# Gate matrices of an expert layer: a new loop order in their eviction, and a new placing of the products with u around them

## The chip, the cores and the metric

The kernel runs on one core of a Trainium2 chip. The metric is device time in microseconds of one launch. The kernel before was timed three times: 2685.2, 2690.42 and 2691.59 us, median 2690.42.

## The reference, cut to what matters

Two transformer layers work on 256 latent tokens and 256 context tokens of width 1024. Each has attention heads and then an expert network of 16384 experts (PEER). Layer 1 runs its experts on the 256 latent tokens alone. This is the expert part:

```
q = (xb @ wq).reshape(T, HEADS=8, 2, 128)
s = einsum('thpd,pnd->thpn', q, sub_keys)          # 2 x 128 scores per head
sv, si = top_k(s, 16)
cand = sv[:, :, 0, :, None] + sv[:, :, 1, None, :] # 256 pairs per head
fv, fp = top_k(cand, 16)
eidx = take_along_axis(cidx, fp)                   # 16 experts per token and head
g = softmax(fv)
a = einsum('thkd,td->thk', take(u, eidx), xb)
wgt = gelu(a) * g
out = einsum('thk,thkd->td', wgt, take(v, eidx))
```

An expert's number is i * 128 + j, so that a token's chosen experts and their softmax weights can be written as a 128 by 128 gate matrix, mostly zero.

## The kernel before, in words

In both layers most token tiles take a dense way through the experts. Layer 0 has four tiles of 128 tokens: three go the dense way (nd = 3), and the fourth gathers single rows of u and v by GpSimd while the main loop runs. Layer 1 has two tiles, both dense (nd = 2).

The dense way has four stages, all in `peer` (lines 991 to 1208) and what it calls.

1. **Scores** (`route_scores`, line 808). Sixteen query blocks are projected with wq, multiplied with the sub-keys, and VectorE takes the top 16 of each. SyncE loads the weights into six raw buffers (tag w) and every one is split into a rounded high and a low part: ScalarE casts (line 166), VectorE subtracts (line 167). A product of two split operands is three matmuls (lines 190 to 192). Weight loads follow one list, `start_weights`; `w_end` bounds how far down it `take` may load ahead. In layer 0 it ends behind the adaLN blocks that the filler uses.
2. **Prologue.** `route` (line 856, six steps per tile, almost all VectorE) finds a tile's 128 experts (i, j) and weights. `gates` (line 919) then makes the gate matrices of 128 tokens, eight tokens at a time: VectorE compares with an iota for the one-hot tiles oh (line 946) and weighs them into og (lines 949, 952; ScalarE does the rest of og, line 956), TensorE multiplies the pairs (line 970), and ScalarE evicts each PSUM tile p of four tokens t by 128 j into `stage`, which is laid out [128 rows, 128 j, 32 t] (line 973). SyncE stores a full stage to G in DRAM by two transfers of 1024 KB (line 977).
3. Meanwhile **chunks** of u run: `achunk` (line 1027) multiplies 128 experts of u with all dense tokens, 24 matmuls in the split form, followed by a Gelu into `ring` (line 1039). In layer 1 every fifth chunk is taken unsplit (line 212). `lag` chunks (27 in layer 0, 47 in layer 1) are done before the main loop. A chunk loads u up to three chunks ahead and splits one ahead. The adaLN products (line 244) are a filler in layer 0.
4. **Main loop**, 128 rounds: loads v and G, does one more chunk of u while there are any, multiplies ring with the gates (line 1167), splits the result w and v, and accumulates w times v (lines 190 to 192 on vs, w) in PSUM.

How many chunks go where in the prologue is paced by weights: a route step of any tile counts RW = 3, a half step of gates 1, and chunk i is issued once `i * tot < done * (lag - TAIL[l])`. Counted through, layer 0 issues 3 chunks during the first tile's route steps, 20 during gates, and 4 behind them; layer 1 issues 6, 36 and 5. The chunks left over come before the filler is drained, before the last pool is closed and before the main loop's `load_g(0)`, `load_v(0)`, `load_v(1)`.

[...]

Of the kernel before, what the change touches and what calls it, by code (L numbers as in the profile page):

```python
# [15 lines left out]
AF = mybir.ActivationFunctionType  # L16
# [12 lines left out]
LAG = (27, 47)  # L29
LATE = 12  # L30
RW = 3
ADA_LOAD = 3
AV1 = 2
EARLY = (2, 1)
# [3 lines left out]
GPIPE = 2  # L38
FSTEP = 3
GSCALE = 16384.0  # L40
TAIL = (4, 5)
RSTEP = 4
U_AHEAD = (1, 3)
RAWQ = (3, 6, 9, 12, 15)
# [45 lines left out]
class Kernel:  # L90
# [34 lines left out]
    def start_weights(self):  # L125
        A = self.A
        q = []
        for half in range(2):
            for v in (0, 1):
                q += self.ada_specs(0, v)[4 * half:4 * half + 4]  # L130
            q += [(("win", b), A["ab_in"][b], 1024, True) for b in ((0, 1), range(2, 14))[half]]
        q += [(("av", b), A["ab_v"][b], 1024, True) for b in range(4)]
        for v in (2, 3, 4):
            q += self.ada_specs(0, v)
        q += [(("wout0", b), A["w_out"][0, b], 1024, True) for b in range(8)]
        q += [(("wq0", b), A["wq"][0, b], 1024, True) for b in range(16)]
        q += self.ada_specs(0, 5)
        for v in range(AV1):
            q += self.ada_specs(1, v)
        self.w1_at = len(q)  # L140
        q += [(("cdin", 0), A["cd_in"][0], 1024, True)]
        q += [(("ckv", b), A["cd_ckv"][b], 768, True) for b in range(4)]
        q += [(("cdin", b), A["cd_in"][b], 1024, True) for b in range(1, 9)]
        q += [(("dv", b), A["cd_v"][b], 1024, True) for b in range(4)]
        q += [(("uq", 0), A["uq_n"], 1024, True), (("uq", 1), A["uq_r"], 512, True), (("ukv", 0), A["ukv"], 1024, True)]
        for v in range(AV1, 6):
            q += self.ada_specs(1, v)
        q += [(("wout1", b), A["w_out"][1, b], 1024, True) for b in range(8)]
        q += [(("wq1", b), A["wq"][1, b], 1024, b not in RAWQ) for b in range(16)]
        self.wq_, self.wl, self.wsp, self.wt = q, 0, 0, 0  # L150
        self.wraw, self.whi = {}, {}
        self.w_end = self.w1_at

    def ada_specs(self, l, v):
        return [(("ada", l, b), self.A["ada_w"][l, b], 1024, False) for b in range(8 * v, 8 * v + 8)]
# [649 lines left out]
        for v, y, p in zip(V, b, X):  # L805
            nc.vector.max_index(p[:, 8:16], v[:, 8:16], y)

    def route_scores(self, l, T, nd, hh, hl):

        nc = self.nc  # L810
        kt = self.wn.t("rt", [128, 2, 128], name="kt")
        nc.sync.dma_start(kt, self.A["keys"][l])
        sv = [self.wn.t("rt", [128, 2, 2, 16, 16], name="sv") for _ in range(nd)]
        sd = self.dp.tile([128, 16, 128], F, name="sd") if T > nd else None
        qs = {}
        c = T * 128
        ready = {}

        def project(b):
            p = self.proj_t(("wq%d" % l, b), hh, hl, c=c)  # L820
            q = self.wn.t("rt", [128, 512], name="q")
            nc.scalar.copy(q[:, :c], p[:, :c])
            qs[b] = q

        def scores(b):
            q = qs.pop(b)
            p = self.ps([128, 4, 128])
            for t in range(T):
                nc.tensor.matmul(p[:, t, :], q[:, t * 128:(t + 1) * 128], kt[:, b % 2, :], start=True, stop=True)
            s = self.wn.t("rt", [128, 2, 4, 128], name="sc")  # L830
            nc.scalar.copy(s[:, 0, :T, :], p[:, :T, :])
            if T > nd:
                nc.sync.dma_start(sd[:, b, :], s[:, 0, nd, :])
            ready[b] = s

        def top(b):
            s = ready.pop(b)
            self.top16([x[:, 0, 0, b, :] for x in sv], [x[:, 0, 1, b, :].bitcast(U32) for x in sv],
                       [s[:, 0, t, :] for t in range(nd)], [s[:, 1, t, :] for t in range(nd)])

        routes = [self.route(x, lambda n, s, d=F: self.wn.t("rt", s, d, name=n)) for x in sv]
        for b in range(18):
            if b == 10:
                for r in routes[:EARLY[l]]:
                    next(r)
            if b < 16:
                project(b)
            if 0 <= b - 1 < 16:
                scores(b - 1)
            if 0 <= b - 2 < 16:  # L850
                top(b - 2)
        return routes, sd
# [67 lines left out]
    def gates(self, go, ti, G):  # L920

        nc = self.nc
        p = self.ps([128, 3, 128])
# [35 lines left out]
        def product():  # L959
            n, oh, og_ = pend.pop(0)  # L960
            part, q = n // 4, n % 4
            if q == 0:
                stages[part] = self.wn.t("stage", [128, 128, 32])
            stage = stages[part]
            for half in range(2):
                p = self.ps([128, 4, 128])
                for k in range(4):
                    for w in range(2):
                        g, b = half * 2 + k // 2, k % 2
                        nc.tensor.matmul(p[:, k, :], oh[:, 0, g, :, b], og_[:, w, g, :, b], start=(w == 0),  # L970
                                         stop=(w == 1))
                c4 = q * 8 + half * 4
                nc.scalar.activation(stage[:, :, c4:c4 + 4].rearrange("p i t -> p t i"), p, AF.Copy,  # L973
                                     scale=1.0 / GSCALE)
            if q == 3:
                for c in range(2):
                    nc.sync.dma_start(G[16 * c:16 * c + 16, :, 4 * ti + part, :, :].rearrange("c p i t -> p c (i t)"),
                                      stage[:, 64 * c:64 * c + 64, :].rearrange("p (c i) t -> p c (i t)", i=4))
# [9 lines left out]
    def peer(self, l, xs, sq, nd):  # L988
# [13 lines left out]
        self.m.close()  # L1002
        rg = Phase(self.tc, "ring%d" % l, {"ring": lag + 2})
        self.wn = Phase(self.tc, "win%d" % l, W_BUFS)
        routes, sd = self.route_scores(l, T, nd, hh, hl)
        G = self.dp.tile([32, 128, 4 * nd, 4, 32], F, name="G%d" % l)
        self.rt = []
        ustr, usp, useen, vstr, gstr, ring = {}, {}, set(), {}, {}, {}
# [1 line left out]
        def load_u(i):  # L1010
            if i < NCH and i not in useen:
                useen.add(i)
                ustr[i] = self.wraw_t()
                nc.sync.dma_start(ustr[i], A["uT"][l, i].rearrange("p k e -> p (k e)"))
# [4 lines left out]
        def split_u(i):  # L1019
            if i < NCH and i not in usp and not raw(i):  # L1020
                h, o = self.wsp_t(), self.wsp_t()
                self.split(ustr.pop(i), h, o)
                usp[i] = (h, o)

        def achunk(i):
            for k in range(U_AHEAD[1] + 1):
                load_u(i + k)
            for k in range(U_AHEAD[0] + 1):
                split_u(i + k)
            p = self.ps()  # L1030
            if raw(i):
                self.product8(p[:, c], ustr.pop(i))
            else:
                uh, ul = usp.pop(i)
                for k in range(8):
                    b = slice(k * 128, (k + 1) * 128)
                    self.mm3(p[:, c], uh[:, b], ul[:, b], hh[:, k, c], hl[:, k, c], k == 0, k == 7)
            ring[i] = rg.t("ring", [128, TD])
            nc.scalar.activation(ring[i], p[:, c], AF.Gelu)


        def prologue():
            for _ in routes[0]:
                yield RW
            for t in range(nd):
                nxt = routes[t + 1] if t + 1 < nd else None
                for n, _ in enumerate(self.gates(self.rt[t], t, G)):
                    yield 1
                    if nxt and n % RSTEP == RSTEP - 1 and next(nxt, True) is None:
                        yield RW  # L1050
                if nxt:
                    for _ in nxt:
                        yield RW

# [5 lines left out]

        filler = fill()
        i = 0
        tot = (6 * nd - EARLY[l]) * RW + nd * (32 + 2 * GPIPE)
        done = 0
        for n, w in enumerate(prologue()):
            done += w
# [2 lines left out]
            while i < lag and i * tot < done * (lag - TAIL[l]):  # L1069
                achunk(i)  # L1070
                i += 1
        while i < lag:
            achunk(i)
            i += 1
        for _ in filler:
            pass
        self.wn.close()
# [63 lines left out]
        def load_v(i):  # L1141
            if i < NCH:
                vstr[i] = mn.t("v", [128, 1024])
                nc.sync.dma_start(vstr[i], A["v"][l, i * 128:(i + 1) * 128, :])

        def split_v(i):
            if i < NCH:
                h, o = mn.t("vs", [128, 1024], R), mn.t("vs", [128, 1024], R)
                self.split(vstr[i], h, o)
                vstr[i] = (h, o)  # L1150

        def load_g(i):
            if i < 32:
                gstr[i] = mn.t("g", [128, 4 * nd, 4, 32])
                nc.sync.dma_start(gstr[i], G[i])
# [34 lines left out]
            return min(256, -(-256 * (at(j + 1) - at(LATE)) // (at(NCH - 3) - at(LATE))))  # L1190

        nu = 0
        load_g(0)
        load_v(0)
        load_v(1)
        split_v(0)
        weight(0)
        for j in range(NCH):
# [277 lines left out]
```

## Time and profile before

| what | value |
|---|---|
| median of three runs | 2690.42 us |
| profiled execution | 2690.64 us |
| its span, first to last instruction | 2688.9 us |
| TensorE busy (PE) | 2574.6 us, 96% |
| VectorE busy (DVE) | 1870.6 us, 70% |
| ScalarE busy (ACT) | 1266.4 us, 47% |
| mean granted TensorE clock | 0.981 |

How to read it: an engine is busy while one of its instructions executes. TensorE's matmuls overlap in the records, so the step from one start to the next tells its pace better than a matmul's duration. An idle stretch of an engine is put down to the event that ended it. [...]

### The profile page before, as it was taken

The page shows a single profiled execution, that of the slowest core. Times are in us where ns is not written, and L with a number is a line of the kernel's source. Part 1 is how long each engine was busy: PE and PEld are TensorE (multiplying, and loading weights), DVE is VectorE, ACT ScalarE, POOL GpSimd, SP SyncE. Part 2 cuts the span into 40 slices and gives each one's busy share as a digit, 9 for nine tenths or more (in the row PEclk, how much of TensorE's full clock was granted, in tenths as well). Part 3 has the DMA queues.
Part 4 walks back from the last instruction along what each step waited for, and adds up shares of the span by engine and source line. Part 5 has one row for each costly group of instructions (what it writes and reads, how often), then busy time and mean ns, then how long its engine had stood idle before and what let it go on. Part 6 is the DMA issues. An engine that isn't in the chain of part 4 may idle for free. (4 is left out here: it accounts for less than half of the span.)

```text
span 2688.9 us, 43066 instructions
## 1 busy us (share of the span) xinstructions
PE 2574.6 (96%) x16265; PEld 2248.1 (84%) x16265; DVE 1870.6 (70%) x3862; ACT 1266.4 (47%) x2201; POOL 526.7 (20%) x534
## 2 busy tenths in 40 slices
PE   7999998989999999999999997999999999999998
PEld 6866787878999999999999777768999899999986
DVE  4267689886967777777777756477987665555555
ACT  4255335996333333333333334454599444444444
POOL 0000000000045555556666631010000000000000
PEclk9999999989999999999999998999999999999999
DMA  7362324877688888888888863464478876666355
GB/s 295 104 220 99 110 89 143 283 236 243 233 312 311 310 314 312 300 319 314 304 301 306 277 227 110 156 218 144 136 248 247 314 256 212 211 211 212 126 196 180
DMA packets 240977, 614.15 MB, mean 228 GB/s; under 512 B 18384, under 2 KB 102608, under 8 KB 240768
## 3 DMA queue, kind: packets, MB, share of 16 engines
q1 hardware_dynamic: 203904, 477.17, 52.0%
q0 software_dynamic: 36864, 134.23, 14.2%
q8 instruction: 127, 2.08, 0.3%
q14 instruction: 82, 0.67, 0.1%
HBM read 558.90 MB, written 52.43 MB: 227 GB/s over the span
## 5 line engine op out<-in xcount | busy, mean ns | idle before, releaser
L166 ACT CAST ws<-w 128x1024 fp32r<-128x1024 f32 (+1 forms) x327 | 342.9, 1050 | 632.7 <-PE p L191 584.0
L167 DVE TENSOR_TENSOR ws<-w,ws 128x1024 fp32r<-128x1024 f32 (+1 forms) x327 | 397.4, 1216 | 262.9 <-ACT ws L166 256.7
L166 ACT CAST vs<-v 128x1024 fp32r<-128x1024 f32 x256 | 269.5, 1053 | 506.5 <-PE p L191 506.5
L191 PE MATMUL p<-vs,w 128*128 128x512 f32 x1280 | 502.3, 393 | 5.2 <-DVE vs L167 5.2
L190 PE MATMUL p<-vs,w 128*128 128x512 f32 x1280 | 499.6, 391 | 5.0 <-ACT vs L166 5.0
L192 PE MATMUL p<-vs,w 128*128 128x512 f32 x1280 | 501.3, 392 | 0.0
L190 PE MATMUL p<-hh,ws 128*128 128x384 f32 (+1 forms) x1304 | 462.2, 355 | 6.3 <-ACT ws L166 2.9
L192 PE MATMUL p<-hh,ws 128*128 128x384 f32 (+1 forms) x1304 | 455.7, 350 | 1.6 <-DVE ws L167 1.6
L191 PE MATMUL p<-hl,ws 128*128 128x384 f32 (+1 forms) x1304 | 456.6, 350 | 0.1
L167 DVE TENSOR_TENSOR vs<-v,vs 128x1024 fp32r<-128x1024 f32 x256 | 312.7, 1222 | 152.2 <-ACT vs L166 149.2
L190 PE MATMUL p<-hp,ws 128*128 128x256 f32 x1032 | 295.7, 287 | 1.8 <-ACT ws L166 1.1
L192 PE MATMUL p<-hp,ws 128*128 128x256 f32 x1032 | 293.0, 284 | 0.8 <-DVE ws L167 0.8
L191 PE MATMUL p<-hp,ws 128*128 128x256 f32 x1032 | 293.4, 284 | 0.0
L191 PEld LDWEIGHTS p<-vs,w 128*128 128x128 f32 x1280 | 241.2, 189 | 53.7 <-DVE vs L167 8.4
L192 PEld LDWEIGHTS p<-vs,w 128*128 128x128 f32 x1280 | 240.9, 188 | 53.3 <-DVE w L1169 2.4
L190 PEld LDWEIGHTS p<-vs,w 128*128 128x128 f32 x1280 | 241.1, 189 | 51.4 <-ACT vs L166 5.3
L190 PEld LDWEIGHTS p<-hh,ws 128*128 128x128 f32 x1304 | 247.9, 190 | 24.7 <-ACT ws L166 4.4
L191 PEld LDWEIGHTS p<-hl,ws 128*128 128x128 f32 x1304 | 247.7, 190 | 14.7 <-DVE hl L367 0.3
L192 PEld LDWEIGHTS p<-hh,ws 128*128 128x128 f32 x1304 | 247.3, 190 | 13.1 <-DVE ws L167 2.0
L1139 DVE SCALAR_TENSOR_TENSOR acc<-gr,ga,acc 128x1024 f32<-128x1024 f32 x128 | 164.2, 1283 | 100.8 <-DMA gr<-in_v,ix 100.0
L1134 DVE SCALAR_TENSOR_TENSOR gr<-gr,hn 128x1024 f32<-128x1024 f32 x128 | 156.0, 1222 | 107.7 <-DMA gr<-in_u,ix 107.4
L310 POOL TENSOR_TENSOR rso<-rsm,mhalf 128x1 f32<-128x1 f32 x30 | 20.2, 673 | 1055.0 <-DVE rsm L308 1041.6
(273 smaller groups left out, 4118.5 us busy)
## 6 DMA issues: line engine op xcount, KB each, us to landing
w<-in_uT SPq DMA_DIRECT2D x256, 512.0 KB
v<-in_v SPq DMA_DIRECT2D x256, 512.0 KB
w<-in_ada_w SPq DMA_DIRECT2D x96, 512.0 KB
G<-stage SPq DMA_DIRECT2D x40, 1024.0 KB
g<-G SPq DMA_DIRECT2D x32, 768.0 KB
w<-in_wq SPq DMA_DIRECT2D x32, 512.0 KB
g<-G SPq DMA_DIRECT2D x32, 512.0 KB
w<-in_w_out SPq DMA_DIRECT2D x16, 512.0 KB
```

The costliest lines, as they stand in the source:

```text
L166: self.nc.scalar.copy(hi, raw)
L167: self.nc.vector.tensor_tensor(lo, raw, hi.bitcast(F), op=OP.subtract)
L190: m(out, lh, rh, start=start, stop=False)
L191: m(out, lh, rl, start=False, stop=False)
L192: m(out, ll, rh, start=False, stop=stop)
L310: nc.gpsimd.tensor_tensor(o, m, self.mhalf[:, :n], op=OP.pow)
L1134: nc.vector.scalar_tensor_tensor(t, t, 1.0, hn, op0=OP.mult, op1=OP.mult, accum_out=ga[:, 0, n:n + 1])
L1139: nc.vector.scalar_tensor_tensor(acc, t, ga[:, 0, n - 128:n - 127], acc, op0=OP.mult, op1=OP.add)
```

## The change

- Line 973's eviction writes `stage` in its own order, four tokens side by side for each j, and reads the PSUM tile with a stride of 128 words from token to token. Before, it read the PSUM tile in order and wrote single words 32 words apart.
- `route_scores` calls `ahead(b)` after each projection: from b = 14 on it loads one chunk of u per step, and at b = 17 it splits chunk 0. In layer 0 the weight list is bounded at `late_at`, ahead of the filler's adaLN blocks, until the scores are done.
- Route steps of the first tile count 8 (layer 0) and 5 (layer 1) in the pacing, and TAIL of layer 1 is 8. Counted through, layer 0 issues 6 chunks in the first tile's route steps, 18 during gates and 3 behind them; layer 1 issues 9, 30 and 8.
- The chunks left over are issued after the filler's drain, the closing of the pool, `load_v(0)`, `load_v(1)` and `load_g(0)`, in this order; the two v loads come ahead of `load_g(0)`.

```diff
+RW0 = (8, 5)
-TAIL = (4, 5)
+TAIL = (4, 8)
 def start_weights
         q += [(("wq0", b), A["wq"][0, b], 1024, True) for b in range(16)]
+        self.late_at = len(q)
         q += self.ada_specs(0, 5)
...
-        self.w_end = self.w1_at
+        self.w_end = self.late_at
 def route_scores(self, l, T, nd, hh, hl, ahead)
             if b < 16:
                 project(b)
+            ahead(b)
 def gates
-                nc.scalar.activation(stage[:, :, c4:c4 + 4].rearrange("p i t -> p t i"), p, AF.Copy,
+                nc.scalar.activation(stage[:, :, c4:c4 + 4], p.rearrange("p t i -> p i t"), AF.Copy,
                                      scale=1.0 / GSCALE)
 def peer
-        routes, sd = self.route_scores(l, T, nd, hh, hl)
...
+        def ahead(b):
+            if b >= 14:
+                load_u(b - 14)
+            if b == 17:
+                split_u(0)
+
+        routes, sd = self.route_scores(l, T, nd, hh, hl, ahead)
+        if l == 0:
+            self.w_end = self.w1_at
...
             for _ in routes[0]:
-                yield RW
+                yield RW0[l]
...
-        tot = (6 * nd - EARLY[l]) * RW + nd * (32 + 2 * GPIPE)
+        tot = (6 - EARLY[l]) * RW0[l] + 6 * (nd - 1) * RW + nd * (32 + 2 * GPIPE)
...
-        while i < lag:
-            achunk(i)
-            i += 1
         for _ in filler:
             pass
...
-        load_g(0)
         load_v(0)
         load_v(1)
+        load_g(0)
+        while i < lag:
+            achunk(i)
+            i += 1
         split_v(0)
         weight(0)
```

## Rows read from the trace of the kernel before

**Rows 1.** The page's first part: busy time, share of the span, instructions.
```profile
PE 2574.6 (96%) x16265; PEld 2248.1 (84%) x16265; DVE 1870.6 (70%) x3862; ACT 1266.4 (47%) x2201; POOL 526.7 (20%) x534
```

**Rows 2.** Layer 0 by stretch: start:end length, busy of PE PEld DVE ACT POOL, PEclk, DMA.
```profile
411.00:440.00 29.00, 20.01 (x168) 17.98 (x171) 27.82 (x135) 11.65 (x16) 0.53 (x1) 0.87 0.39 131
440.00:634.00 194.00, 170.99 (x1634) 153.95 (x1626) 160.44 (x338) 179.13 (x344) 2.10 (x4) 0.92 0.75 234
634.00:656.50 22.50, 20.39 (x113) 20.07 (x114) 12.26 (x14) 11.98 (x18) 0.00 (x0) 0.92 0.89 303
```

**Rows 3.** Groups of ScalarE instructions from 440 to 634 us: busy us, mean ns | idle before.
```profile
L973 ACT ACTIVATE stage<-p 128x512 f32<-128x512 f32 x96 | 98.0, 1135 | 2.3 <-PE p L970 2.3
L956 ACT ACTIVATE og<-oh,gl 128x128 f16<-128x128 f16 x192 | 62.9, 445 | 2.6 <-DVE oh L946 2.4
L166 ACT CAST ws<-w 128x1024 fp32r<-128x1024 f32 x18 | 19.2, 1073 | 1.6 <-PE p L191 1.6
L1039 ACT ACTIVATE ring<-p 128x384 f32<-128x384 f32 x20 | 10.0, 502 | 4.0 <-PE p L192 4.0
```

**Rows 4.** Groups of VectorE instructions from 440 to 634 us.
```profile
L946 DVE TENSOR_TENSOR oh<-io,ijgt 128x2048 f16<-128x2048 f16 x48 | 58.5, 1218 | 7.2 <-ACT ijgt L928 7.2
L949 DVE TENSOR_TENSOR og<-oh,ijgt 128x1024 f16<-128x1024 f16 x48 | 32.9, 686 | 0.6
L167 DVE TENSOR_TENSOR ws<-w,ws 128x1024 fp32r<-128x1024 f32 x20 | 24.4, 1221 | 15.7 <-ACT ws L166 15.7
L952 DVE TENSOR_TENSOR og<-oh,ijgt 128x512 f16<-128x512 f16 x48 | 20.1, 418 | 0.0
```

**Rows 5.** TensorE's waits in three stretches (411:440, then 440:634, then 1904:2097).
```profile
PE p L228 <- DVE ijg L916: 6.3, 1, 6.3
...
PE p L970 <- DVE og L949: 10.3, 7, 3.2
PE p L970 <- ACT og L956: 6.6, 4, 1.8
...
PE p L190 <- ACT vs L166: 5.0, 1, 5.0
PE p L228 <- DVE ijg L916: 2.9, 1, 2.9
```

**Rows 6.** First and last of ten matmuls of a layer 0 chunk: start us, us.
```profile
430.56 0.33 PE L192 MATMUL p<-hh,ws 128*128 128x384 f32 x1
...
432.12 0.34 PE L192 MATMUL p<-hh,ws 128*128 128x384 f32 x1
```

**Rows 7.** Groups by form, ScalarE over the span, then VectorE from 411 to 660 us.
```profile
L973 ACT ACTIVATE stage<-p 128x512 f32<-128x512 f32 x160 | 164.1, 1143 | 2.5 <-PE p L970 2.3
L478 ACT COPY PT<-p 128x512 f32<-128x512 f32 x32 | 18.7, 586 | 8.0 <-PE p L228 7.7
...
L900 DVE CAST xs<-sv 128x128 f16<-128x128 f32 x3 | 0.8, 258 | 0.0
L889 DVE CAST sv<-sv 128x128 f32<-128x128 uint32 x3 | 0.7, 219 | 0.0
```

**Rows 8.** Layer 1 by stretch, columns as in Rows 2.
```profile
1904.00:1927.00 23.00, 20.03 (x140) 18.68 (x140) 22.96 (x114) 10.28 (x17) 0.00 (x0) 1.00 0.34 115
1927.00:2077.00 150.00, 146.76 (x1367) 141.30 (x1366) 123.95 (x231) 140.99 (x268) 0.00 (x0) 0.99 0.74 230
2077.00:2097.00 20.00, 14.95 (x99) 13.87 (x98) 9.08 (x12) 9.01 (x15) 0.00 (x0) 0.95 0.97 332
```

**Rows 9.** SyncE's queue before layer 1's main loop, then the chain's G load (start, us).
```profile
2076.90 3.50 SPq L977 DMA_DIRECT2D G<-stage  x2
2080.49 4.05 SPq L1014 DMA_DIRECT2D w<-in_uT  x2
2084.64 0.42 SPq L1155 DMA_DIRECT2D g<-G  x1
...
2084.64 6.58 DMA g<-G
```

More of the change, by code (lines that the diff above doesn't have):

```diff
@@ L806, in top16, with route_scores @@
             nc.vector.max_index(p[:, 8:16], v[:, 8:16], y)
-    def route_scores(self, l, T, nd, hh, hl):
+    def route_scores(self, l, T, nd, hh, hl, ahead):
         nc = self.nc
```

## The prediction

> **What bounds the kernel now.** I read the page's first part, then busy time by stretch over both prologues, then the groups and waits inside them. TensorE is busy for 96% of the span [rows 1] and the change takes no matmul away, so only time in which TensorE waits or runs slowly can be won. In the stretches by time the reader should look for two things: which engine is full where TensorE is not, and the granted clock. [...] VectorE's largest idle time is its wait for ScalarE's casts, 15.7 us [rows 4]. TensorE waits for og, 10.3 us for VectorE's part and 6.6 us for ScalarE's [rows 5]. In layer 1's gates TensorE is nearly full, 146.8 of 150 us, with ScalarE at 141.0 just behind [rows 8]. The other losses are single stalls: 6.3 us in layer 0 and 2.9 us in layer 1, where the last chunk of the route steps is done and the first tile's ijg is not, and 5.0 us where layer 1's main loop starts and its first v split has waited on ScalarE behind the G data [rows 5, 9].
>
> **The eviction.** The instruction keeps its 512 elements. A copy of the same size on the same engine, PSUM to SBUF with both sides in order, takes 0.586 us, the eviction 1.143 [rows 7]: the difference of 0.557 us is what single words scattered 128 bytes apart cost. After the change the written side has four adjacent words at a time; the read side hops 512 bytes each element, and no row shows a strided read of PSUM. Bounds: 0.586 from below (the copy); from above 1.70, today's time with the same 0.557 us added once more, since nothing in the trace excludes that a hopping read costs more than a hopping write. The nearest row of a strided read is on VectorE in SBUF: 128 elements read 64 bytes apart take 0.258 us against 0.219 in order [rows 7], 0.04 us more, so 0.16 us for 512. I take 0.70 us, nearest to the copy, a little under 0.586 + 0.16 = 0.75, since that row is of another engine and memory.
>
> The trace shows that scattered single words cost, and not whether four-word runs cure it. [...]
>
> **Layer 0, gates.** ScalarE: 96 x (1.135 - 0.70) = 41.8 us less; two chunks fewer lie in the gates (18 for 20), each a cast of 1.07 and a Gelu of 0.50 [rows 3], 3.1 us. It falls to 179.1 - 41.8 - 3.1 = 134 us. VectorE does the same gates and routes and two subtractions of 1.22 us fewer [rows 4]: 158 us. TensorE: nine matmuls of a chunk start within 1.56 us, 0.173 us apart [rows 6], a chunk of 24 is 4.2 us, so 171.0 x 0.92 - 2 x 4.2, about 149 us at full clock. VectorE is late next, and that is what limits the gain: with ScalarE anywhere under some 0.95 us per eviction (179.1 - 3.1 - 96 x 0.18 = 158) VectorE is the bound. Of the 33.6 us that it idles now I leave 8: half of the wait of 7.2 us on ijgt, which is a chain through TensorE, and a quarter of that on the casts. So the gates last 166 us in place of 194.
>
> Their start moves back by the three more chunks in the route steps. VectorE is full there (27.8 of 29.0 us [rows 2]), so their splits of 1.22 us come on top: 3.7 us. TensorE's 12.6 us for them go into its 6.3 us stall and the wait around it, and cost nothing more unless they outlast the chain, by which the gates would start up to 5 us later; the range holds that. Behind the gates one chunk less is left over, 4.2 us. The stretch from 634 to the first v product at 656.5 is otherwise kept. Layer 0: 3.7 + 166 - 194 - 4.2 = -28 us.
>
> **Layer 1.** The 2.9 us stall is filled by three more chunks, each by estimate 2.8 us (two thirds of layer 0's columns). They overshoot the chain by some 5 us, but as TensorE is the bound of the gates that only orders its work otherwise. In the gates ScalarE has 64 x 0.44 = 28 us less and six chunks fewer, VectorE seven; TensorE's 3.2 us of waits there go [rows 8], and the clock losses of 0.01 x 150 + 0.05 x 20 = 2.5 us that follow the stalls. At the main loop's start the last G store is issued at 2076.90, the G load at 2084.64, and it lands 6.58 us later [rows 9], 14.3 us in all; eight chunks left over are 22 us and cover it, where five with their loads in front did not, so the 5.0 us go. Sum 2.9 + 3.2 + 2.5 + 5.0 = 13.6; I keep 1.6 for waits that reappear, so -12 us.
>
> **The loads.** The u loads in the projections put chunks 0 to 3 ahead of adaLN blocks in the same six buffers. Both come some 6 us apart before they are used, so I take 0, between 2 us gained at the first chunk and 3 us lost at the first filler step. The two v loads now stand ahead of `load_g(0)`, and the leftover chunks' u loads behind it. [...] The last chunk of the prologue has loaded three more chunks (12.5 us of TensorE in layer 0, 8.4 in layer 1), and a later one may be planned ahead of the G load, so I take 0; the price without that cover is the first rival's.
>
> **Sum.** -28 - 12 = -40 us on the profiled execution's 2690.64 us (span 2688.9 and 1.7 around it), which is 0.2 us over the median: 2650 us. Its own range is 2634 to 2668.
>
> **Rivals.**
> 1. *Starved leftover chunks.* The eviction is fast, but u loads stuck behind `load_g(0)` leave TensorE dry. SyncE is held 2084.64 - 2076.90 = 7.7 us [rows 9], then v, v, G and u, some 2 MB at 332 GB/s [rows 8], 6 to 7 us more: 14 us against 8.4 of cover in layer 1 and 12.5 in layer 0, so 6 + 2 us and a slow clock after each, some 4 us. 2662 us. [...] Against: the u issue of 2080.49 stands between G store and G load today, so loads that are ready do get in.
> 2. *The read pays what the write paid.* The eviction stays near 1.14 us and only the placing counts. Layer 0: gates start 3.7 later, ScalarE has 3.1 less in them, one chunk less behind: -3.6. Layer 1: gates start 3 x 2.8 - 2.9 = 5.5 later, ScalarE's bound shrinks by 6 x 1.45 = 8.7, three more chunks behind add 8.4 and hide 5.0: about 0. 2687 us.
> 3. *The read pays more*: the eviction at 1.70 us. ScalarE is the bound of both gates, so every 0.1 us adds 0.1 x 160 = 16 us [rows 7]: -3.4 + 89 gives 2776 us. It decides from 1.21 us on, where the 3.4 us are spent and 8 more are lost. For it: no row shows a read that hops 512 bytes. Against: the one strided read that a row shows costs 0.3 ns per element [rows 7].
>
> **How the numbers follow.** Forecast 0.60, rival 1 0.13, rival 2 0.17, rival 3 0.10. A difference under 0.3%, 8 us, can't be told from no change: within it lies most of rival 2, 0.12, its rest is faster. Faster 0.60 + 0.13 + 0.05 = 0.78, same 0.12, slower 0.10. The range starts at 2632, where VectorE idles nowhere in layer 0's gates (8 us more) and nearly nothing reappears, and ends at 2692, past rival 2; it leaves out rival 3 and a little below.
>
> **What the profile after would show.** The eviction group under 0.95 us, near 0.70. Layer 0's gates at some 166 us with VectorE fuller than ScalarE. No wait of TensorE for ijg in either layer, six and nine chunks ahead of the first transposes. The first v product of layer 1 without a wait for vs. Wrong if the eviction is 1.1 us or more; if it is fast and the gates of layer 0 still last over 180 us; or if TensorE waits for u in the leftover chunks.

## The result, and the profile after

The change made the kernel faster, by less than forecast: 2664.55 us median (2661.32 to 2667.70, four runs) beside 2691.01 of the kernel before on the same chip, 26.5 us, ratio 0.9893 [0.9871, 0.9915]. Forecast were 2650 us and 40 us. In a second set of runs it was 2668.97 beside 2693.58, ratio 0.9918 [0.9892, 0.9945]. The profiled execution is the 2661.32 one.

First the page's busy time, then the eviction's group over the span (line 973 before is 976 now; VectorE's and ScalarE's lines 166/167, 946, 949 are 168/169, 949, 952; TensorE's gate products, 970 before, are 973 now).

```profile
PE 2553.3 (96%) x16265; PEld 2232.6 (84%) x16265; DVE 1868.8 (70%) x3862; ACT 1201.5 (45%) x2201; POOL 514.6 (19%) x534
```

```profile
L976 ACT ACTIVATE stage<-p 128x512 f32<-128x512 f32 x160 | 86.4, 602 | 6.3 <-PE p L973 6.0
```

ScalarE lost 64.9 us of work against [rows 1], and the eviction's group alone lost 77.7: 602 ns for one where [rows 7] have 1143. It is now within 16 ns of the plain copy's 586 in the same rows. The other groups of ScalarE last as long as before; that the sum fell by less than the group is no new work. Instructions of ScalarE overlap in the trace, and the page counts such time once: by count and mean of its groups they last 1448.6 us in sum in the kernel before and 1358.4 now, 90.2 us less, and the busy times are 1266.4 and 1201.5.

The stretches of both prologues come next, in the columns of [rows 2]: layer 0's route steps, gates and the part behind them, then the same of layer 1.

```profile
409.60:437.00 27.40, 27.40 (x211) 26.63 (x210) 27.40 (x122) 11.92 (x15) 0.53 (x1) 1.00 0.52 168
437.00:612.00 175.00, 153.60 (x1576) 138.20 (x1575) 157.73 (x336) 140.22 (x342) 2.10 (x4) 0.95 0.82 251
612.00:633.20 21.20, 18.14 (x109) 17.82 (x109) 9.46 (x10) 10.35 (x16) 0.00 (x0) 0.99 1.01 336
1888.00:1915.60 27.60, 27.58 (x205) 26.55 (x205) 27.24 (x112) 13.25 (x20) 0.00 (x0) 1.00 0.43 153
1915.60:2041.00 125.40, 122.69 (x1202) 118.54 (x1201) 114.95 (x224) 107.06 (x257) 0.00 (x0) 1.00 0.79 245
2041.00:2067.00 26.00, 26.00 (x194) 25.16 (x193) 12.66 (x19) 11.58 (x19) 0.00 (x0) 1.00 1.02 360
```

Against [rows 2] the fullest engine of layer 0's gates has changed: before, it was ScalarE, busy for 179.1 of 194 us, 98.0 of them with the evictions [rows 3]; now VectorE is busy for 157.7 of 175 us, ScalarE for 140.2. In layer 1 [rows 8] TensorE is now busy for all but 2.7 us of 179, and its granted clock (PEclk, as a share of full speed) is 1.00 in all three stretches.

Now the waits in layer 0 from the end of the scores to the main loop, first TensorE's, then VectorE's (one answer for 437:612, one for 612:640), then two of VectorE's in the kernel before (440:634 and 634:660). The figures are us in total, times, longest us.

```profile
PE p L973 <- DVE og L952: 8.5, 8, 2.7
PE p L246 <- DMA w<-in_ada_w: 4.8, 2, 4.1
...
PE p L192 <- ACT w L1177: 3.1, 1, 3.1
```

```profile
DVE mod L275 <- PE p L270: 6.5, 2, 6.0
DVE oh L949 <- ACT ijgt L931: 4.8, 2, 2.7
DVE ws L169 <- ACT ws L168: 1.7, 2, 1.4
...
DVE ws L169 <- ACT ws L168: 9.9, 4, 3.6
DVE vs L169 <- ACT vs L168: 4.6, 1, 4.6
```

```profile
DVE mod L273 <- PE p L268: 3.8, 1, 3.8
...
DVE ws L167 <- ACT ws L166: 14.1, 4, 6.7
```

TensorE's wait for ijg [rows 5] is gone. VectorE's wait for casts inside the gates fell from 15.7 us [rows 4] to 1.7, but one for TensorE grew from 3.8 to 6.5 us, and at the main loop's door VectorE waits for casts as long as before, 14.5 us beside 14.1.

For the comparisons the trace was cut at events: start of the first score product, its end, the first transpose of ijg, the last gate product, the first v product. Each length is the difference of two start times, in us.

| | before | after | after, 2nd | eviction only | placing only |
|---|---|---|---|---|---|
| layer 0, scores | 93.8 | 91.4 | 91.4 | 93.8 | 91.4 |
| to the first ijg transpose | 22.8 | 27.5 | 27.5 | 23.0 | 27.5 |
| to the last gate product | 190.7 | 174.4 | 174.3 | 174.2 | 193.8 |
| to the first v product | 27.1 | 21.8 | 21.6 | 23.0 | 24.4 |
| layer 0, main loop | 955.9 | 961.8 | 965.3 | 970.7 | 965.6 |
| layer 1, scores' end to first v | 190.0 | 178.8 | 179.7 | 181.4 | 191.4 |

Profiled execution against profiled execution 29.3 us went: layer 0's scores 2.4, from there to the first v product 16.9, layer 1's prologue 11.2, its main loop 1.7; the start of the kernel 3.9 shorter, layer 0's main loop 5.9 longer and the way from there to layer 1's scores 0.7 longer.

### The profile page after: what moved, and what is told of

It is laid out like the page before. It is cut to its first block, busy times and chain, and to the rows that moved or that the text cites. A ratio compares the mean times of both kernels' runs of the same rounds, so it can differ in the third digit from the quotient of the medians.

```text
span 2659.5 us, 43074 instructions
## 1 busy us (share of the span) xinstructions
PE 2553.3 (96%) x16265; PEld 2232.6 (84%) x16265; DVE 1868.8 (70%) x3862; ACT 1201.5 (45%) x2201; POOL 514.6 (19%) x534
## 5 line engine op out<-in xcount | busy, mean ns | idle before, releaser
L193 PEld LDWEIGHTS p<-vs,w 128*128 128x128 f32 x1280 | 241.3, 189 | 58.1 <-DVE vs L169 12.8
L1143 DVE SCALAR_TENSOR_TENSOR gr<-gr,hn 128x1024 f32<-128x1024 f32 x128 | 156.0, 1222 | 107.4 <-DMA gr<-in_u,ix 107.0
```

The source lines that it names most:

```text
L193: m(out, lh, rl, start=False, stop=False)
L1143: nc.vector.scalar_tensor_tensor(t, t, 1.0, hn, op0=OP.mult, op1=OP.mult, accum_out=ga[:, 0, n:n + 1])
```

## The experiments

**The changed kernel once more.** The same file.

> The changed kernel once more, as a measure for the others. Profiled before at 2661.3 us with 29 us less than the kernel before: 17 us between the end of layer 0's scores and its first v product, 11 us in layer 1's same stretch, but 6 us more lost in layer 0's main loop, where VectorE waits for gathered rows of v. If that loss belongs to the change, the main loop of layer 0 again takes about 962 us against 956; if it is scatter of the gathers, it falls anywhere between 950 and 965. Time 2660 to 2668.

Measured: 2668.97 us, 1 us over the range expected, ratio 0.9918 [0.9892, 0.9945]. The prologues repeat to 1 us. The start (318.2 and 324.3 us) and layer 0's main loop (961.8 and 965.3, which neither theory gave) don't: a single profile of these two says little.

**The eviction alone**, in the kernel before.

```diff
-  nc.scalar.activation(stage[:, :, c4:c4 + 4].rearrange("p i t -> p t i"), p, AF.Copy,
+  nc.scalar.activation(stage[:, :, c4:c4 + 4], p.rearrange("p t i -> p i t"), AF.Copy,
```

> The kernel before with the new eviction alone. Theory A, ScalarE was the bound of layer 0's gates and the eviction is most of the gain: eviction 0.60 us, layer 0's gates some 15 us shorter, layer 1's 5, the stalls of 6.3 and 2.9 us at the first tile's ijg and the 5.0 us at layer 1's main loop stay: 2668 to 2675. Theory B, the placing is most of it and ScalarE's time was hidden anyway: 2685 or more.

Measured: 2667.41 us, just under theory A's range, ratio 0.9904 [0.9886, 0.9922], which can't be told from the whole change. Theory A holds: by the table layer 0's gates are 16.5 us shorter than before. Its three stretches of layer 0, columns as before:

```profile
413.30:436.30 23.00, 16.76 (x139) 15.51 (x138) 23.00 (x117) 9.15 (x11) 0.53 (x1) 0.88 0.41 144
436.30:611.00 174.70, 159.71 (x1619) 144.62 (x1620) 161.25 (x341) 140.24 (x341) 2.11 (x4) 0.96 0.81 254
611.00:633.50 22.50, 22.50 (x135) 22.18 (x135) 10.87 (x13) 13.80 (x21) 0.00 (x0) 1.00 1.01 336
```

The sums fit that. VectorE is busy for 23.0 + 161.3 + 10.9 = 195.1 us here and for 27.4 + 157.7 + 9.5 = 194.6 in the changed kernel. A chunk moved out of the gates takes its subtraction along to the route steps, where VectorE is full too (busy for all of the 23.0 and of the 27.4 us). TensorE's wait for ijg of 6 us and its clock of 0.88 in the route steps are still there in this kernel and cost nothing that the sum shows: from the scores' end to the first v product it takes 220.2 us, the changed kernel 223.7. So in layer 0 the placing loses some 3 us there, and wins 2.4 in the scores and 2.6 in layer 1's prologue; the two kernels come out even.

**The placing alone**: the changed kernel with the old eviction line (the diff above, reversed).

> The changed kernel with the old eviction (1.14 us). Theory A: ScalarE still bounds the gates, the chunks moved out of them leave TensorE idle there, and the sum is the second rival's 2687 us, within 5 of the kernel before. Theory B: 2670 to 2675, since the stalls at ijg and at the main loop's start are gone.

Measured: 2699.97 us, ratio 1.0026 [1.0009, 1.0042], a few us slower than before, where theory A gave 2687. The eviction is back at its old price, and TensorE's waits between the scores and the main loop are these:

```profile
L976 ACT ACTIVATE stage<-p 128x512 f32<-128x512 f32 x160 | 161.6, 1131 | 5.0 <-PE p L973 4.8
```

```profile
PE p L973 <- ACT og L959: 12.8, 10, 2.0
PE p L973 <- DVE og L952: 6.0, 7, 2.8
PE p L192 <- ACT w L1177: 5.7, 1, 5.7
```

```profile
441.50:636.00 194.50, 166.19 (x1577) 147.38 (x1576) 157.86 (x336) 175.28 (x340) 2.10 (x4) 0.90 0.73 226
```

The last row is the stretch of layer 0's gates. ScalarE does 3.8 us less in it than in [rows 2], as two chunks fewer should give, yet the stretch is no shorter: ScalarE idles 19.2 us where it idled 14.9, and the products wait longer for its og (12.8 us beside 6.6 in [rows 5]). That this comes of fewer chunks between the products is likely, but not shown.

**The loads undone**: no call of `ahead`, and the weight list bounded as before.

```diff
-        self.w_end = self.late_at
+        self.w_end = self.w1_at
...
-            ahead(b)
```

> The changed kernel without the u loads in the projections and with the old end of the weight list. By the prediction both loads come early enough, so the time is the changed kernel's within 2 us and the first ada step does not move. Rival: u loads in front of the adaLN blocks make a later adaLN step wait for its blocks (4.1 us of TensorE at 483 us, with VectorE waiting 6.0 us behind it), then without them that wait goes and the time is 3 to 5 us lower.

Measured: 2675.45 us, ratio 0.9942 [0.9920, 0.9964], 6.5 and 10.9 us above the two sets of the changed kernel, though its interval still overlaps that of the second. Layer 0's scores take 94.5 us in place of 91.4 and the gates' products 170.3 in place of 166.8. ScalarE at the scores' end (start, duration, idle before it):

```profile
410.62 1.05 ACT L168 CAST ws<-w 128x1024 fp32r<-128x1024 f32 x1 [4.25 <-DMA w<-in_uT]
411.57 0.58 ACT L824 COPY q<-p 128x512 f32<-128x512 f32 x1
412.05 0.59 ACT L833 COPY sc<-p 128x512 f32<-128x512 f32 x1
416.54 1.04 ACT L168 CAST ws<-w 128x1024 fp32r<-128x1024 f32 x1 [3.90 <-DMA w<-in_uT]
```

Twice here a cast of a u chunk comes ahead of the copy of q, having waited 4.25 and 3.90 us for its load, and the copy starts 0.95 us behind it; TensorE's longest wait for q is 2.8 us, and the last scores come late. In the kernel before the product for q has ended by 411.21 us, the cast starts at 413.24 after 3.91 us of wait for its load, q's copy at 414.19, and TensorE waits 2.7 us for it. With the early loads its longest wait for q is 0.8 us. TensorE's rows show this wait for a transfer under q, not under the transfer's name. Why the gates' products take longer, too, was not traced. The rival failed: TensorE's wait for the adaLN blocks is still there.

```profile
PE p L246 <- DMA w<-in_ada_w: 4.7, 2, 4.0
```

**Less VectorE work**: for half of the tokens the low part of og (48 instructions of 0.42 us in layer 0) and its products are left out.

```diff
-  nc.vector.tensor_tensor(og_[:, 1, :d], oh[:, 1, :d], bc(3, c)[:, :d], op=OP.mult)
```

> The changed kernel without VectorE's part of the low half of og (line 952 of the kernel before); it leaves out the low part of the weights of half the tokens, with their products. VectorE has 48 x 0.418 = 20 us less in layer 0's gates. Theory V, VectorE bounds layer 0's whole stretch from the scores' end to the first v product (busy 194.6 of 223.5 us, whether 3 or 6 chunks come first): the stretch shrinks by 15 to 20 us and the time to about 2652. Theory Q, waits on transfers behind SyncE's queue and the chain at a tile's first gates fill the 28 us that VectorE idles: under 5 us.

Measured: 2651.53 us, ratio 0.9843 [0.9812, 0.9875]. For 20 us less on VectorE the gates' products took 151.7 us in place of 166.9, and the way from the scores' end to the first v product 210.9 in place of 223.6. The time is theory V's; the way shrank by 12.7 us, less than its 15 to 20. By itself the run doesn't show that VectorE was the bound: a fourth of the gate products, some 13 us of TensorE by the 16 that take 1.08 us in the trace, went as well.

**The same work on GpSimd.**

```diff
-  nc.vector.tensor_tensor(og_[:, 1, :d], oh[:, 1, :d], bc(3, c)[:, :d], op=OP.mult)
+  nc.gpsimd.tensor_tensor(og_[:, 1, :d], oh[:, 1, :d], bc(3, c)[:, :d], op=OP.mult)
```

> The changed kernel with that same part of og done by GpSimd, which is idle in the prologues; nothing is left out. Theory V: if GpSimd takes under some 1.5 us for each of the 48 and VectorE's own instructions keep their 1.22 and 0.69 us, layer 0's stretch shrinks by 12 to 20 us: 2650 to 2657. Rival: GpSimd and VectorE slow each other in SBUF, oh and og take longer than before, and the time is that of the changed kernel or more.

Measured: 2691.18 us, ratio 0.9998 [0.9981, 1.0014]; the whole gain is gone. The groups over the span:

```profile
L955 POOL TENSOR_TENSOR og<-oh,ijgt 128x512 f16<-128x512 f16 x80 | 135.3, 1694 | 265.0 <-DVE oh L949 120.2 <-DMA w<-in_uT 94.1 <-DVE ijgt L933 14.6
L949 DVE TENSOR_TENSOR oh<-io,ijgt 128x2048 f16<-128x2048 f16 x80 | 122.1, 1526 | 6.3 <-ACT ijgt L931 6.3
...
L952 DVE TENSOR_TENSOR og<-oh,ijgt 128x1024 f16<-128x1024 f16 x80 | 69.7, 871 | 1.6
```

What VectorE gave away came back as longer instructions: oh 1526 ns where the changed kernel has 1222, og's high part 871 where it has 687, so 80 x (0.304 + 0.184) = 39 us more for 80 x 0.42 = 33.5 less. The means hide two kinds: by the timeline 29 of the 80 oh instructions took 2.06 us, the others 1.20 to 1.48, and each of the 29 started while a GpSimd multiply was under way. Two of them in a row, then layer 0's gates:

```profile
499.57 1.21 DVE L949 TENSOR_TENSOR oh<-io,ijgt 128x2048 f16<-128x2048 f16 x1
...
500.87 1.54 POOL L955 TENSOR_TENSOR og<-oh,ijgt 128x512 f16<-128x512 f16 x1 [1.30 <-DVE mod L275]
501.43 2.06 DVE L949 TENSOR_TENSOR oh<-io,ijgt 128x2048 f16<-128x2048 f16 x1
```

```profile
441.80:631.00 189.20, 158.79 (x1571) 144.19 (x1569) 177.11 (x288) 141.07 (x342) 80.46 (x52) 0.91 0.75 233
```

Other VectorE instructions got longer as well: in layer 0's gates VectorE is busy for 19.4 us more than in the changed kernel, ScalarE for 0.9, and they last 14.2 us longer with all of TensorE's work kept. With the run before, that speaks for VectorE as the bound, though TensorE now also waits 7.0 us for GpSimd's og. What slows VectorE beside GpSimd, SBUF as the rival has it or something else, the run does not show.

**Both kernels without the gathers** of layer 0's fourth tile and what uses them.

```diff
 def gather(n0, n1, after=None)
-            n1 = min(n1, 256)
...
+            return
 def use(n)
+            return
```

> The kernel before without the fourth tile's gathers and what VectorE does with the gathered rows (left out). With the next run it tells how much of the change's gain layer 0's main loop gives back. The loop without waits is by matmul pace 101 x 8.24 + 27 x 4.08 = 942 us, before it took 956: about 2677.

> The changed kernel without the same. Theory G, the gathers' waits in the last third of the main loop give back some 6 to 9 us of the gain (962 and 965 us in two profiles, 956 before): main loop 942 to 945 as in the run above, and the difference of the two is 30 us or more, against 25 to 26 with gathers. Theory S, that loss is scatter: the difference stays at 25 to 26.

Measured: 2679.63 us, ratio 0.9942 [0.9922, 0.9963], and 2649.59, ratio 0.9834 [0.9811, 0.9858]. The gathers' waits cost both kernels some 10 to 18 us in that loop (945.5 and 947.8 us without them; the 942 expected take a round of it as 24 matmuls 0.173 us apart and 18 matmuls 0.227 us apart, as in the kernel before). By the medians the two are 30.0 us apart, the 30 that theory G wanted, beside 26.5 and 24.6 with the gathers. But the ratios' intervals overlap, 0.9834 over 0.9942 being 0.9891 beside 0.9893 and 0.9918, and the changed kernel's loop is 2.3 us longer without any gather, too. These runs don't settle whether the gathers give back part of the gain.

**A gentler pace of row additions in the main loop.**

```diff
-                return i + min(i, NCH - lag)
+                return 5 * i + 7 * min(i, NCH - lag)
```

> The changed kernel; only the main loop's pace differs: a u round weighs 2.4 of the rounds behind it instead of 2, so that fewer row additions that need gathers (25 rather than 30 of the 1024-wide ones by counting the plan) fall into the last 27 rounds of a layer's main loop, where VectorE waits longest on gathers. Theory G (the crowded last rounds give back part of the gates' gain): layer 0's main loop falls from 962-965 us to about 955, layer 1's likewise by a few us, the kernel to 2655 (ratio about 0.987), and TensorE's waits for vs in the last third fall from 8-10 us to under 5. Rival (the waits on gathers come from the gathers themselves, wherever they lie, or the u rounds now run into VectorE's limit): main loop 962-966 or longer, kernel 2665 or more.

Measured: 2662.59 us, ratio 0.9884 [0.9857, 0.9911]; main loop 958.4 us. The time lies between the two theories, and its interval holds the first ratio of the unpaced kernel, 0.9893, and overlaps the second's. The waits fell as theory G wanted, the loop less. TensorE's waits for vs from 1400 us on, first this kernel, then the changed one:

```profile
PE p L193 <- DVE vs L169: 4.4, 3, 2.0
```

```profile
PE p L193 <- DVE vs L169: 8.5, 5, 3.3
```

**The eviction in pairs** in place of fours.

```diff
-  nc.scalar.activation(stage[:, :, c4:c4 + 4], p.rearrange("p t i -> p i t"), AF.Copy,
+  nc.scalar.activation(stage[:, :, c4:c4 + 4].rearrange("p i (a t) -> p a i t", t=2),
+                       p.rearrange("p (a t) i -> p a i t", t=2), AF.Copy,
```

> The changed kernel with the same eviction in two-word runs instead of four-word runs, the read of PSUM strided as before it. If a pair of adjacent words suffices for full rate on ScalarE, as runs of four do, the eviction takes 0.60 us as in the changed kernel and the gates stay at 167 us. If ScalarE needs runs longer than a pair, it lies between 0.60 and 1.14 us; if the longer access pattern itself costs, a little over 0.60, by estimate up to 0.65.

Measured in one run: 2661.54 us.

```profile
L976 ACT ACTIVATE stage<-p 128x512 f32<-128x512 f32 x160 | 91.8, 643 | 6.0 <-PE p L973 5.8
```

643 ns: nearly all of the gain comes with the second adjacent word, and 41 ns more with the fourth; whether those are the run's length or the longer access pattern is not told apart. The gates' products took 169.4 us, 2.5 more than with fours. The main loop, with the fast gates, lasted 957.9 us.

**The kernel before once more.**

> The kernel before, unchanged, for the scatter of its stretches: whether layer 0's main loop lasts 955.9 us again. Theory G, by which the changed kernel's 961.8 and 965.3 us there are a loss that the change brings, wants 954 to 958. If it lies at 960 to 966, the main loop's difference between the two kernels is scatter between executions and no loss, and the shortfall of the forecast lies in the gates and behind them alone.

Measured in one run: 2693.29 us; main loop 958.0 us. By itself that is what theory G wanted. The other profiles don't bear it out: 957.9 us with fast gates (pairs), 965.6 and 965.4 with slow ones (placing alone, GpSimd), 970.7 with the eviction alone. Gates' speed and main loop's length don't go together. The profiles with gathers lie up to 15 us apart there, two of one kernel 2.1 and 3.5 us; six launches of the changed kernel in one set took 2662.2 to 2679.65 us. So scatter is likely, but a loss of a few us stays possible and was not settled.

**A version meant to beat both**: the pace, one chunk moved from the route steps behind the gates, and a little of og's low part from VectorE to ScalarE in layer 0.

```diff
-AGRP = (2,)
+AGRP = ((2, 2, 3), (2,))
-TAIL = (4, 8)
+TAIL = (5, 8)
```

> The changed kernel with three small edits: in layer 0's gates every third build gives one more group of the low part (two tokens) from VectorE to ScalarE (15 builds, by rows of the changed kernel VectorE 15 x 0.21 = 3.1 us less, ScalarE 30 x 0.44 = 13 us more, so both near 154 us); TAIL of layer 0 is 5 for 4, which moves one chunk from the route steps behind the gates (5, 18, 4 for 6, 18, 3); and the main loop's pace as in the run before. Theory V (VectorE is the bound of layer 0's gates, and ScalarE has room since the eviction is fast): route steps about 1 us shorter, gates about 3 us shorter, the wait of 3.1 us for the first w gone while one chunk of 4.2 us more stands there, so from the end of the scores to the first v product 219 to 220 us instead of 223.5; with the pace 2657 to 2660. Rival (ScalarE's added work delays its evictions and casts, and TensorE waits for them): gates 167 us or longer and 2663 or more.

Measured: 2663.17 us, ratio 0.9890 [0.9870, 0.9910], no better than the changed kernel. From the scores' end to the first v product it took 228.1 us, and the gates' products 172.2, so the rival's numbers held, but not its reason: TensorE waits 0.8 us for ScalarE's og there and 18.2 for VectorE's. Layer 0's gates, then VectorE's largest wait in them:

```profile
437.80:616.60 178.80, 155.90 (x1568) 140.24 (x1569) 156.25 (x339) 143.60 (x364) 2.64 (x5) 0.93 0.79 241
```

```profile
DVE ws L169 <- ACT ws L168: 10.1, 2, 8.5
```

VectorE did 1.5 us less and took 3.8 us more. One wait for a cast, 8.5 us, undid the shift: ScalarE's cast itself waited (5.1 us) for a buffer that TensorE still read. VectorE is the fullest engine of these gates, but not the only bound; here a cast that waits for one of the three pairs of split buffers came right behind it. The pace comes after the gates and left them alone in the run with it; which of the other two edits brought the stall was not told apart.

## Why the prediction was right, and where its size was off

**The eviction: right.** 0.602 us; taken were 0.70, the bounds 0.586 and 1.70. In the forecast any value under 0.95 gave the same sum, so the error of 0.1 us cost nothing there; with the pairs, 41 ns slower, the gates' products took 2.5 us longer in one profile, so ScalarE's time was not quite without weight. Runs of two bring nearly all of the gain: 643 ns beside 602 for fours and 1131 to 1143 for single words. No row of before has a strided read of PSUM; the forecast's 0.16 us for it were an estimate from a row of VectorE, and the eviction with that read takes 16 ns more than the copy in order.

**The bound that comes next: right, its idle time too small.** VectorE's 157.7 us in layer 0's gates are the 158 forecast, and ScalarE's 140 the 134. The step that failed is "I leave 8" of VectorE's 33.6 us of idle time: 17.3 stayed. The two waits of which it kept a part came out in sum much as it had them: the casts left 1.7 us of 15.7 and the wait for ijgt 4.8 of 7.2, together 6.5 where 7.5 were kept. What it put at nothing without a reason was the rest: the wait of `mod` for TensorE, 3.8 us before and 6.5 now, and 4.3 us of a small wait and of gaps too short for the list. The wait of `mod` is a late weight load of the adaLN filler: TensorE waits 4.8 us for in_ada_w, VectorE then for TensorE. That wait is 2.7 us in the kernel before, 2.6 with the eviction alone, 4.9 with the placing alone, 4.7 without the early loads, and 2.8 again in the version that moves one chunk: it goes with where the chunks stand, not with the loads. So the gates took 175 us, not 166. The stretch of 194 us in [rows 2] also runs 4.6 us past the last gate product; cut at the events the gates went from 190.7 to 174.4, 16.3 us.

**The route steps and the leftover chunks: right in kind, but not to be added.** Forecast +3.7 in front and -4.2 behind, measured +4.7 and -5.3, and in the latter stands a stall of 3.1 us for the first w that was not foreseen. ScalarE behind the gates shows its origin:

```profile
627.55 1.05 ACT L168 CAST vs<-v 128x1024 fp32r<-128x1024 f32 x1 [4.43 <-DMA v<-in_v]
...
632.64 0.51 ACT L1177 CAST w<-ring 128x384 fp32r<-128x384 f32 x1 [1.77 <-DVE ring L1176]
```

```profile
606.18 10.94 SPq L980 DMA_DIRECT2D G<-stage  x4
617.21 4.04 SPq L1016 DMA_DIRECT2D w<-in_uT  x2
621.35 0.96 SPq L1153 DMA_DIRECT2D v<-in_v  x2
```

In SyncE's queue (second fence) the stores of G take until 617.12 and two loads of u until 621.25, and v is issued at 621.35; its cast starts at 627.55, and the first weights follow the splits on VectorE. It looks like rival 1's held queue, with v in place of u, and at 3 us; but the DMA share of that stretch is 1.01, and no run tells the queue from full DMA engines. The eviction alone shows that the two cancel: VectorE's work between the scores and the main loop is the same with the chunks in either place (195.1 and 194.6 us).

**Layer 0 in sum:** from the scores' end -28 forecast, -16.9 measured. The loads, costed at 0 within 2 gained and 3 lost, brought 2.4 us in the scores and 3.5 in the gates: a gain outside those bounds.

**Layer 1: right in its sum, less so in its terms.** -11.2 us up to the first v product and 1.7 in its main loop, -12 forecast. The stall for ijg and that for vs are gone. But the forecast had 7.9 of its 13.6 us from these two stalls, which the placing was to cure, and the eviction alone brought 8.6 us with the first of them kept and most of the second gone:

```profile
PE p L228 <- DVE ijg L916: 2.9, 1, 2.9
PE p L190 <- ACT vs L166: 1.2, 1, 1.2
```

The placing added 2.6 us to that (178.8 beside 181.4), and by itself lost 1.4. That the sum came out is in part luck.

**The rivals.** Rival 1 did not come for u. SyncE's queue before layer 1's main loop (start, us; x: instructions):

```profile
2041.37 3.67 SPq L980 DMA_DIRECT2D G<-stage  x2
2045.14 4.74 SPq L1016 DMA_DIRECT2D w<-in_uT  x2
2049.97 0.86 SPq L1153 DMA_DIRECT2D v<-in_v  x2
2050.92 0.60 SPq L1164 DMA_DIRECT2D g<-G  x1
2051.61 0.96 SPq L1016 DMA_DIRECT2D w<-in_uT  x1
```

The G load is issued 9.6 us after the last stores, not 7.7 as [rows 9] had it, and u's follow it at once; no row has TensorE waiting for u. The 4 us that it adds for a slow clock come from no row that it names; in the kernel before the granted clock was 0.50 for 3.4 us, a loss of 1.7, soon after each of layer 1's stalls of 2.9 and 5.0 us: from 1927.6 and from 2094.85 us on. Rival 2's premise fell with the eviction; run by itself, the placing came out at 2700 us, where 2687 were worked out for it. That sum had 3.6 us won in layer 0 from the scores' end; by the table 5.1 were lost. It counted ScalarE's lighter work as time won and left out that its idle time would grow. Rival 3 fell with the eviction as well.

**The size in sum.** Of 40 us forecast the stretches in question gave 2.4 + 16.9 + 11.2 + 1.7 = 32.2 in the profiles. The medians gave 26.5, the ratio's interval 23 to 35. So 7.8 us are missing there, all of them in layer 0, where VectorE's idle time in the gates alone is 9.3 us over the forecast; of the other 5.7 no run tells a loss from scatter. The lower end of the range, 2632 us, doesn't follow from the terms named for it (8 and 1.6 us under 2650); nothing hung on it.

## What to carry to other kernels

Once the fullest engine of a stretch is relieved, count the next one's work over the whole stretch up to the next serial point, and keep most of its present waits: here VectorE's wait for ScalarE's casts fell from 15.7 us to 1.7 in layer 0's gates, and its wait for TensorE rose from 3.8 to 6.5. Work moved between stretches that share that bound moved the time here and did not shorten it (VectorE busy for 195.1 and 194.6 us). And price a load by the engine on which its consumer stands: here a cast waited 4.25 us for its load, and the copy of q came behind it.

## What the runs showed of the hardware

On ScalarE, 512 words from PSUM to SBUF took 586 ns in order, 602 with the read 128 words apart and runs of four written, 643 with runs of two, 1131 to 1143 with single words written 32 words apart and the read in order: in these times the order of the writes weighs more than that of the reads. GpSimd took 1694 ns in the mean for a 128x512 f16 multiply that VectorE does in 418 (the changed kernel). VectorE's own f16 instructions beside it took 25 to 27% longer in the mean, but not evenly: 29 of 80 comparisons took 2.06 us in place of 1.22, all of them started during a GpSimd multiply, and the others 1.20 to 1.48.
